# Turning the gated products of the first layer with VectorE and transfers through DRAM, and another order of the first stage's transfers, in a two-layer trunk

## The chip, the cores and the metric

The kernel runs on one core of a Trainium2 chip. The metric is the device time of one execution in microseconds. The engines are named as the profile names them: PE (TensorE, its weight loads apart as PEld), DVE (VectorE), ACT (ScalarE), POOL (GpSimd) and SP (SyncE); the last two only issue transfers here.

## The reference, cut to what matters

One sequence of T = 256 tokens with D = 2048 goes through two layers, all in float32. Layer 0 mixes tokens with an mLSTM, layer 1 with forgetting attention (FoX). Each layer also has a feed-forward part with 5632 hidden columns, and each of the two parts of a layer is preceded by a normalisation that is modulated by numbers worked out from a conditioning vector c:

```python
cs = jax.nn.silu(c)
for layer in range(DEPTH):
    mod = cs @ ada_w[layer] + ada_b[layer]
    sh1, sc1, g1, sh2, sc2, g2 = split(mod, 6)
    h = rms_norm(x, norm_mix_w[layer]) * (1.0 + sc1) + sh1
    y = mlstm_mixer(h) if layer == 0 else fox_mixer(h)
    x = x + g1 * y
    h = rms_norm(x, norm_ffn_w[layer]) * (1.0 + sc2) + sh2
    g, u = jnp.split(h @ w_gate_up[layer], 2, axis=-1)
    x = x + g2 * ((jax.nn.silu(g) * u) @ w_down[layer])
return rms_norm(x, final_norm_w)
```

The change touches two places: how silu(g) * u, which comes out with tokens on the partitions, gets its hidden columns onto the partitions for the product with w_down in layer 0; and the first stage, where mod, h and the first product with the mixer's weights are begun.

## The kernel before, in words

**Matmuls.** Every weight matrix is read once, in tiles of 4 rows of 128 (k) by 512 columns, 1 MB each, by `fetch` (L252) on SP's queue into one of five buffers (`rawp`). To keep float32 accuracy each tile is split, two rows at a time: ACT casts the high part (`hi`, L261), DVE subtracts it from the tile for the low part (`lo`, L262), and PE does three matmuls for each row and each half of the tokens: high activations by high weights (L288), high by low (L289), low by high (L290). Such a split of two rows feeds 12 matmuls; its two results have four buffers each. The activations lie as tiles with the contracted dimension on the partitions, a high part in the first 256 columns and a low one in the next 256.

**Modulation.** The 2 x 6 x 16 rows of `ada_w` come in tiles of 1 MB (L192) on the same queue and into the same five buffers; DVE multiplies each with silu(c) and sums it (L193). In the first stage the tiles for the scale and the shift of layer 0's first norm are taken in the order written there; all later ones are background work (`want`, `bg`), released by a credit that grows at each fetched weight tile by the stage's rate. Gate rows are turned and broadcast over the partitions through DRAM by POOL's queue (`grow`, L402 and L410).

**Steps.** Small work is appended to a list, `steps`, and `tick`, which runs once per fetched weight tile (4 rows of k), takes one step from it. `drain` takes several at once.

**The feed-forward part (`ffn`).** The hidden columns are taken in 11 groups of 512, in two chunks: groups 0 to 5, then the product with their rows of `w_down`, then groups 6 to 10 and the rest of `w_down`. In a group (`swiglu`) the gate column goes through Silu on ACT (L1116), the up column's product is taken by DVE from PSUM (L1119), and then come the steps that turn the 256 x 512 result into four activation tiles, in two halves by `flip(0)` and `flip(1)`: a copy of the high part by ACT (L1147) and a subtraction for the low part by DVE (L1148). How these two see the turned data differs by layer. In layer 0 `turned` does four 128 x 128 transposes on PE into a PSUM bank (L345) in each flip. In layer 1 (`TURN`) six steps stand in place of two: `turn(0)` and `turn(1)`, each a DVE transpose of 32 x 32 squares in place (L1128) with a 256 KB store to DRAM (`aside`) on POOL's queue (L1132); `spread`, four loads from there that set the squares in place (L1136, into `whole`); an empty step; and the two flips, which read SBUF.

In layer 0 the first halves (in k) of 11 columns of the first chunk have been summed before the norm was complete (`nsplit`), so a group there has four ticks; otherwise it has eight. At the end of a chunk `ffn` runs what is left of the steps: all of them in layer 0, all but three in layer 1. The rest goes with the ticks of the product with `w_down`, before whose last fetched tile the list is emptied.

**The first stage.** The first four columns of the mixer's input product (`FIRST`) begin while the modulation is still being worked out. For the first three rows of k the weights and activations are used whole (`full_k`, L785, 16 matmuls for each row), from pairs of rows of 512 KB (`fetch_pair`, L780); the fourth row is split (`split_last`, L797 and L798). `early` is a generator that goes from modulation tile to modulation tile: `upto(k)` runs it until the norm's row k - 1 is written. `norm_full` writes such a row: DVE scales (L737), ACT adds the shift (L741), ACT and DVE split it (`split_act`, L362 and L363).

Of the kernel before, what the change touches and what calls it, by code (L numbers as in the profile page):

```python
# [9 lines left out]
F32 = mybir.dt.float32  # L10
# [3 lines left out]
ALU = mybir.AluOpType  # L14
# [4 lines left out]
T = 256  # L19
# [12 lines left out]
def kernel(  # L32
# [5 lines left out]
    nc = tc.nc  # L38
# [77 lines left out]
    hT = const.tile([P, KT, 2 * T], F32R, name="hT")  # L116
# [72 lines left out]
    def ada_tile(layer, vec, k):  # L189
        j = 16 * vec + k  # L190
        raw = rawp.tile([P, D], F32, tag="raw", name=nm("ada"))
        nc.sync.dma_start(raw, ada_w[layer, j])  # L192
        nc.vector.scalar_tensor_tensor(  # L193
            out=raw, in0=raw, scalar=1.0, in1=cs, op0=ALU.mult, op1=ALU.mult,
            accum_out=acc[layer][:, j : j + 1],
        )
# [164 lines left out]
    def split_act(src, dst):  # L361
        nc.scalar.copy(dst[:, :T], src)  # L362
        nc.vector.tensor_tensor(dst[:, T:], src, dst[:, :T].bitcast(F32), op=ALU.subtract)  # L363
# [366 lines left out]
    FIRST, N2 = CFG["first"], CFG["n2"]  # L730
    full = {}

    def norm_full(k):
        a = mods[0][:, 16 * SC1 + k : 16 * SC1 + k + 1]
        b = mods[0][:, 16 * SH1 + k : 16 * SH1 + k + 1]
        t1 = t256()
        nc.vector.scalar_tensor_tensor(  # L737
            out=t1, in0=xT[k], scalar=a, in1=R, op0=ALU.mult, op1=ALU.mult
        )
        full[k] = f = t256()  # L740
        nc.scalar.activation(f, t1, AF.Identity, bias=b)  # L741
        split_act(f, hT[:, k, :])

    def early():
        for k in range(KT):
            for vec in (SC1, SH1):
                ada_tile(0, vec, k)
                if k == 0 and vec == SC1:
                    row_scale()
                set_mods(0, vec, k, 1)  # L750
                if vec == SC1:
                    yield
            if k < 4:
                norm_full(k)
            else:
                norm_tile(k, 0, SC1, SH1)
            at[0] = k + 1
            yield

    at = [0]  # L760
    gen = early()

    def upto(k):
        while at[0] < k:
            next(gen)
# [12 lines left out]
    def fetch_pair(i, k):  # L778
        raws[i, k // 2] = raw = slot().rearrange("p (k c) -> p k c", c=512)
        nc.sync.dma_start(raw, w[COLS[i] // 512, 0, :, k : k + 2, :])  # L780

    def full_k(k):
        for i in range(FIRST):
            for t in range(2):
                nc.tensor.matmul(  # L785
                    vbanks[i][t], full[k][:, t * P : (t + 1) * P], raws[i, k // 2][:, k % 2, :],
                    start=k == 0, stop=False, skip_group_check=True,
                )

    def split_last(i):  # L790
        if i % 2 == 0:
            fine[i // 2] = [
                splitp.tile([P, 2, 512], F32R, tag=g, name=nm(g)) for g in ("hi", "lo")
            ]
        hi, lo = (h[:, i % 2, :] for h in fine[i // 2])
        src = raws[i, 1][:, 1, :]
        nc.scalar.copy(hi, src)  # L797
        nc.vector.tensor_tensor(lo, src, hi.bitcast(F32), op=ALU.subtract)  # L798
        pairs.append((hi, lo))

    fine, pairs = {}, []
    upto(1)
    for i in range(FIRST):
        fetch_pair(i, 0)
    full_k(0)
    upto(2)
    full_k(1)
    upto(3)
    for i in range(2):
        fetch_pair(i, 2)  # L810
        split_last(i)
    upto(4)
    for i in range(2, FIRST):
        fetch_pair(i, 2)
        split_last(i)
    full_k(2)
    for i in range(FIRST):
        mm_a(vbanks[i], *pairs[i], h_act(3), False, True)
# [248 lines left out]
    begun = project_out(w_out, res, LR[4], 1, 8, norm, gate_up[0], [0, DFF, 512])  # L1067


    TURN = (1,)  # L1070

    def pair(t):
        return t.rearrange("p (t c) -> p t c", t=2)
# [321 lines left out]
```

## Time and profile before

| | |
|---|---|
| median of 3 runs | 2287.39 us (2287.02 to 2288.49) |
| the profiled execution | 2287.58 us |
| its span in the trace | 2285.6 us |
| granted TensorE clock, mean | 0.999 |
| DMA, mean over the span | 278 GB/s, 635.44 MB |
| the first matmuls of L288 | from 44.59 us |
| products (L1119) of layer 0's first chunk | 563.52 to 690.44 us |
| products of layer 0's second chunk | the last transposes after it end at 1044.9 us |

Times in the rows of a view are microseconds from the start of the span. A row of a timeline has the start, the duration, the engine, the line, the operation, the tile written and the tiles read, and how many instructions in a row it stands for; in brackets is the idle time of the engine before it and what ended this. A row of the groups has the busy time, the mean of one in ns, and the idle time before all of them. PE's matmuls overlap, so the duration of one is longer than the step from one to the next.

### The profile page before, as it was taken

The page shows a single profiled execution, that of the slowest core. Times are in us where ns is not written, and L with a number is a line of the kernel's source. Part 1 is how long each engine was busy: PE and PEld are TensorE (multiplying, and loading weights), DVE is VectorE, ACT ScalarE, POOL GpSimd, SP SyncE. Part 2 cuts the span into 40 slices and gives each one's busy share as a digit, 9 for nine tenths or more (in the row PEclk, how much of TensorE's full clock was granted, in tenths as well). Part 3 has the DMA queues.
Part 4 walks back from the last instruction along what each step waited for, and adds up shares of the span by engine and source line. Part 5 has one row for each costly group of instructions (what it writes and reads, how often), then busy time and mean ns, then how long its engine had stood idle before and what let it go on. Part 6 is the DMA issues. An engine that isn't in the chain of part 4 may idle for free.

```text
span 2285.6 us, 26531 instructions
## 1 busy us (share of the span) xinstructions
PE 2259.6 (99%) x10290; PEld 1853.0 (81%) x10290; DVE 1642.5 (72%) x1855; ACT 1133.3 (50%) x1493; POOL 53.8 (2%) x106
## 2 busy tenths in 40 slices
PE   8999999999999999999999999999999999999998
PEld 4877878888888888888888888888888888888886
DVE  7998789878877877865687777777666555555564
ACT  4778564555543344444554544455444443444443
POOL 1000000000000000000000000000010100010000
PEclk9999999999999999999999999999999999999999
DMA  9998989798888889985567878675787665566662
GB/s 386 369 354 332 350 307 355 281 342 336 324 330 332 323 332 342 340 299 185 212 251 277 310 261 293 240 271 195 256 288 254 221 204 189 198 226 217 206 228 104
DMA packets 91809, 635.44 MB, mean 278 GB/s; under 512 B 10962, under 2 KB 11410, under 8 KB 17316
## 3 DMA queue, kind: packets, MB, share of 16 engines
q1 hardware_dynamic: 86400, 617.79, 73.9%
q0 software_dynamic: 5136, 15.83, 2.4%
q8 instruction: 80, 1.31, 0.2%
q14 instruction: 45, 0.37, 0.0%
q10 hardware_dynamic: 148, 0.14, 0.0%
HBM read 625.82 MB, written 7.90 MB: 277 GB/s over the span
## 4 chain that ended last, share of the span: by engine, by line
PE 87%; DVE 6%; DMA 4%; ACT 2%; issue 1%; SPq 0%; POOL 0%; ACTq 0%; DVEq 0%; POOLq 0%
PE mm L290 25%; PE mm L289 25%; PE mm L288 25%; PE mm L271 5%; DMA ada<-in_ada_w_dram 3%; DVE ada L193 3%; PE mm L274 3%; DVE lo L262 2%; ACT hi L261 1%; PE aux L345 1%; PE aux L974 0%; PE aux L483 0%; PE aux L1201 0%; PE mm L554 0%; PE mm L550 0%
## 5 line engine op out<-in xcount | busy, mean ns | idle before, releaser
L262 DVE TENSOR_TENSOR lo<-raw,hi 128x1024 fp32r<-128x1024 f32 x764 | 925.7, 1223 | 488.6 <-ACT hi L261 487.9
L261 ACT CAST hi<-raw 128x1024 fp32r<-128x1024 f32 x764 | 795.6, 1052 | 881.3 <-PE mm L290 780.7
L289 PE MATMUL mm<-lo,hT 128*128 128x512 f32 x1846 | 721.1, 391 | 4.5 <-DVE lo L262 4.5
L288 PE MATMUL mm<-hi,hT 128*128 128x512 f32 x1846 | 720.4, 392 | 1.3 <-ACT hT L362 1.3
L290 PE MATMUL mm<-hi,hT 128*128 128x512 f32 x1846 | 720.8, 390 | 0.0
L193 DVE SCALAR_TENSOR_TENSOR ada<-ada,cs 128x2048 f32<-128x2048 f32 x192 | 438.9, 2286 | 52.4 <-DMA ada<-in_ada_w_dram 52.0
L289 PEld LDWEIGHTS mm<-lo,hT 128*128 128x128 f32 x1846 | 346.9, 188 | 79.1 <-DVE lo L262 8.6
L288 PEld LDWEIGHTS mm<-hi,hT 128*128 128x128 f32 x1846 | 346.6, 188 | 73.5 <-ACT hT L362 2.1
L290 PEld LDWEIGHTS mm<-hi,hT 128*128 128x128 f32 x1846 | 346.7, 188 | 72.7 <-issue 0.5
L288 PE MATMUL mm<-hi,slot 128*128 128x512 f32 x960 | 375.5, 391 | 0.2 <-ACT slot L1007 0.2
L289 PE MATMUL mm<-lo,slot 128*128 128x512 f32 x960 | 374.6, 390 | 0.0
L290 PE MATMUL mm<-hi,slot 128*128 128x512 f32 x960 | 374.6, 391 | 0.0
L290 PEld LDWEIGHTS mm<-hi,slot 128*128 128x128 f32 x960 | 180.3, 188 | 37.8 <-issue 0.7
L288 PEld LDWEIGHTS mm<-hi,slot 128*128 128x128 f32 x960 | 180.3, 188 | 37.7 <-ACT slot L1007 0.8
L289 PEld LDWEIGHTS mm<-lo,slot 128*128 128x128 f32 x960 | 180.4, 188 | 36.9
L271 PE MATMUL mm<-hT,hi 128*128 128x512 f32 x512 | 181.8, 402 | 0.9 <-DVE slot L357 0.9
L274 PE MATMUL mm<-hT,lo 128*128 128x256 f32 x512 | 138.4, 281 | 0.0
L271 PEld LDWEIGHTS mm<-hT,hi 128*128 128x128 f32 x512 | 94.5, 188 | 20.8 <-DVE slot L357 1.3
L274 PEld LDWEIGHTS mm<-hT,lo 128*128 128x128 f32 x512 | 96.8, 189 | 3.1
L829 ACT ACTIVATE slot<-mm 128x512 f32<-128x512 f32 x78 | 45.2, 595 | 39.2 <-PE mm L290 37.4
L1148 DVE TENSOR_TENSOR slot<-slot,slot 128x512 fp32r<-128x512 f32 x22 | 23.8, 1089 | 24.1 <-ACT slot L1147 24.1
L433 ACT ACTIVATE t<-X 128x512 f32<-128x512 f32 x32 | 20.1, 629 | 38.4 <-DVE X L428 38.4
(220 smaller groups left out, 1034.1 us busy)
## 6 DMA issues: line engine op xcount, KB each, us to landing
ada<-in_ada_w_dram SPq DMA_DIRECT2D x192, 1024.0 KB, 6.5
raw<-in_gate_up_dram SPq DMA_DIRECT2D x176, 1024.0 KB, 5.0
raw<-in_down_dram SPq DMA_DIRECT2D x88, 1024.0 KB, 4.8
raw<-in_fox_in_dram SPq DMA_DIRECT2D x48, 1024.0 KB, 4.9
raw<-in_w_in_dram SPq DMA_DIRECT2D x44, 1024.0 KB, 7.4
raw<-in_w_out_dram SPq DMA_DIRECT2D x16, 1024.0 KB, 6.5
raw<-in_fox_out_dram SPq DMA_DIRECT2D x16, 1024.0 KB, 4.9
aside<-slot POOLq DMA_DIRECT2D x22, 256.0 KB, 2.7
```

The costliest lines, as they stand in the source:

```text
L193: nc.vector.scalar_tensor_tensor(out=raw, in0=raw, scalar=1.0, in1=cs, op0=ALU.mult, op1=ALU.mult, accum_out=acc[layer][:, j : j + 1],)
L261: nc.scalar.copy(hi, raw[:, j : j + 2, :])
L262: nc.vector.tensor_tensor(lo, raw[:, j : j + 2, :], hi.bitcast(F32), op=ALU.subtract)
L271: nc.tensor.matmul(ps, hi, rhs, start=first, stop=last, skip_group_check=True)
L274: nc.tensor.matmul(ps[:, T:], lo, rhs[:, :T], start=False, stop=False, skip_group_check=True)
L288: nc.tensor.matmul(ps, a, hi, start=first, stop=False, skip_group_check=True)
L289: nc.tensor.matmul(ps, a, lo, start=False, stop=False, skip_group_check=True)
L290: nc.tensor.matmul(ps, b, hi, start=False, stop=last, skip_group_check=True)
L345: nc.tensor.transpose(ps[:, j * T + t * P : j * T + (t + 1) * P], src[:, t, (2 * i + j) * P : (2 * i + j + 1) * P], ident,)
L433: nc.scalar.activation(t512(), X[:, t, 512 * i : 512 * (i + 1)], AF.Square, accum_out=self.ss[:, t, i : i + 1],)
L829: nc.scalar.activation(SP[i][:, t, :], banks[t], func)
L1148: nc.vector.tensor_tensor(dst[:, :, T:], ps, dst[:, :, :T].bitcast(F32), op=ALU.subtract)
```

## The change

It does two things. First, `TURN` holds both layers: layer 0's gated products are turned by DVE and through DRAM as layer 1's are, with six steps a group in place of two, and three steps are left over at the end of a chunk. Second, the first stage is written in another order. The second and third pairs of modulation tiles are asked for between the first weight pairs rather than behind all four of them, and the next ones between the pairs of the third and fourth row. The low parts of the first rows of the norm are put off (`lows`, `lower`) behind the next modulation tile on DVE, and `split_last` becomes `high_last` and `low_last`. The new file's lines move: what was L1116, L1119, L1128, L1132, L1136, L1147 and L1148 is now L1137, L1140, L1149, L1153, L1157, L1168 and L1169; L780 and L785 are L791 and L796, L797 and L798 are L807 and L811, and the subtraction of `norm_full` is L744 in place of L363.

SP's queue at the start, from the second modulation tile pair's predecessors on (`ada` are modulation tiles, `slot` the weight pairs), before and now:

```order
L780 DMA slot_242<-in_w_in_dram 128x1024
L780 DMA slot_244<-in_w_in_dram 128x1024
L780 DMA slot_246<-in_w_in_dram 128x1024
L780 DMA slot_248<-in_w_in_dram 128x1024
L192 DMA ada_258<-in_ada_w_dram 128x2048
L192 DMA ada_262<-in_ada_w_dram 128x2048
L192 DMA ada_280<-in_ada_w_dram 128x2048
L192 DMA ada_284<-in_ada_w_dram 128x2048
L780 DMA slot_294<-in_w_in_dram 128x1024
L780 DMA slot_300<-in_w_in_dram 128x1024
L192 DMA ada_304<-in_ada_w_dram 128x2048
L192 DMA ada_308<-in_ada_w_dram 128x2048
```

```order
L791 DMA slot_241<-in_w_in_dram 128x1024
L791 DMA slot_243<-in_w_in_dram 128x1024
L192 DMA ada_245<-in_ada_w_dram 128x2048
L791 DMA slot_250<-in_w_in_dram 128x1024
L192 DMA ada_252<-in_ada_w_dram 128x2048
L791 DMA slot_261<-in_w_in_dram 128x1024
L192 DMA ada_279<-in_ada_w_dram 128x2048
L192 DMA ada_284<-in_ada_w_dram 128x2048
L791 DMA slot_293<-in_w_in_dram 128x1024
L192 DMA ada_295<-in_ada_w_dram 128x2048
L791 DMA slot_300<-in_w_in_dram 128x1024
L192 DMA ada_308<-in_ada_w_dram 128x2048
```

The third and fourth modulation tile stood behind four weight pairs and now behind two and three; the fifth and sixth keep their place, and the seventh stands ahead of the second pair of the third row.

DVE at the same place, around the third row of the norm (L737), before and now:

```order
L193 SCALAR_TENSOR_TENSOR ada_284,acc_124<-ada_284,cs 128x2048
L187 TENSOR_TENSOR mods_122<-acc_124,prm 128x1
L737 SCALAR_TENSOR_TENSOR t_47_288<-slot_130,mods_122,R 128x256
L363 TENSOR_TENSOR hT<-t_48_290,hT 128x256
L798 TENSOR_TENSOR lo_297<-slot_294,hi_296 128x512
L798 TENSOR_TENSOR lo_297<-slot_300,hi_296 128x512
L193 SCALAR_TENSOR_TENSOR ada_304,acc_124<-ada_304,cs 128x2048
```

```order
L193 SCALAR_TENSOR_TENSOR ada_284,acc_124<-ada_284,cs 128x2048
L187 TENSOR_TENSOR mods_122<-acc_124,prm 128x1
L737 SCALAR_TENSOR_TENSOR t_47_288<-slot_130,mods_122,R 128x256
L193 SCALAR_TENSOR_TENSOR ada_295,acc_124<-ada_295,cs 128x2048
L744 TENSOR_TENSOR hT<-t_48_290,hT 128x256
L181 SCALAR_TENSOR_TENSOR mods_122<-acc_124,prm 128x1
L811 TENSOR_TENSOR lo_303<-slot_293,hi_302 128x512
```

The next modulation tile (L193) comes ahead of the row's low part, and ahead of the low parts of the first two weight rows (L798, now L811).

DVE at the end of layer 0's first chunk: the products of group 5 (L1119, now L1140) and the flips around them (L1148, now L1169). `lo` are weights' low parts; in the second piece `slot_4982` and `slot_5152` are the turned data of groups 3 and 4, `slot_4984` and `slot_5154` the products of groups 4 and 5:

```order
L262 TENSOR_TENSOR lo_5443<-raw_5440,hi_5442 128x1024
L262 TENSOR_TENSOR lo_5447<-raw_5440,hi_5446 128x1024
L193 SCALAR_TENSOR_TENSOR ada_5545,acc_125<-ada_5545,cs 128x2048
L1119 TENSOR_TENSOR slot_5167<-mm_5271,slot_5167 128x512
L1119 TENSOR_TENSOR slot_5167<-mm_5272,slot_5167 128x512
L262 TENSOR_TENSOR lo_5480<-raw_5477,hi_5479 128x1024
L262 TENSOR_TENSOR lo_5484<-raw_5477,hi_5483 128x1024
L1148 TENSOR_TENSOR slot_5422<-aux_5423,slot_5422 128x2x256
L1148 TENSOR_TENSOR slot_5430<-aux_5431,slot_5430 128x2x256
```

```order
L262 TENSOR_TENSOR lo_5443<-raw_5440,hi_5442 128x1024
L193 SCALAR_TENSOR_TENSOR ada_5474,acc_125<-ada_5474,cs 128x2048
L1169 TENSOR_TENSOR slot_5410<-slot_4982,slot_5410 128x2x256
L1169 TENSOR_TENSOR slot_5413<-slot_4982,slot_5413 128x2x256
L1149 STREAM_TRANSPOSE slot_5151<-slot_4984 128x4x4x32 x2
L262 TENSOR_TENSOR lo_5447<-raw_5440,hi_5446 128x1024
L1140 TENSOR_TENSOR slot_5154<-mm_5248,slot_5154 128x512
L1140 TENSOR_TENSOR slot_5154<-mm_5249,slot_5154 128x512
L262 TENSOR_TENSOR lo_5480<-raw_5477,hi_5479 128x1024
L262 TENSOR_TENSOR lo_5484<-raw_5477,hi_5483 128x1024
L193 SCALAR_TENSOR_TENSOR ada_5551,acc_125<-ada_5551,cs 128x2048
L262 TENSOR_TENSOR lo_5517<-raw_5514,hi_5516 128x1024
```

Before, no squares stand there and a flip reads PSUM (`aux`). Now the flips of group 3 and the squares of group 4 (L1149) stand ahead of the second split of the first tile of `w_down` (`lo_5447`), and group 4's flips come six rows after that tile's last, behind the products of group 5.

The diff:

```diff
--- before.py
+++ after.py
@@ -739,12 +739,23 @@
         )
         full[k] = f = t256()
         nc.scalar.activation(f, t1, AF.Identity, bias=b)
-        split_act(f, hT[:, k, :])
+        dst = hT[:, k, :]
+        nc.scalar.copy(dst[:, :T], f)
+        lows.append(lambda: nc.vector.tensor_tensor(
+            dst[:, T:], f, dst[:, :T].bitcast(F32), op=ALU.subtract
+        ))
+
+    lows = []
+
+    def lower():
+        while lows:
+            lows.pop(0)()
 
     def early():
         for k in range(KT):
             for vec in (SC1, SH1):
                 ada_tile(0, vec, k)
+                lower()
                 if k == 0 and vec == SC1:
                     row_scale()
                 set_mods(0, vec, k, 1)
@@ -787,32 +798,42 @@
                     start=k == 0, stop=False, skip_group_check=True,
                 )
 
-    def split_last(i):
+    def high_last(i):
         if i % 2 == 0:
-            fine[i // 2] = [
+            fine.append([
                 splitp.tile([P, 2, 512], F32R, tag=g, name=nm(g)) for g in ("hi", "lo")
-            ]
-        hi, lo = (h[:, i % 2, :] for h in fine[i // 2])
-        src = raws[i, 1][:, 1, :]
-        nc.scalar.copy(hi, src)
-        nc.vector.tensor_tensor(lo, src, hi.bitcast(F32), op=ALU.subtract)
-        pairs.append((hi, lo))
-
-    fine, pairs = {}, []
+            ])
+        pairs.append([h[:, i % 2, :] for h in fine[-1]])
+        nc.scalar.copy(pairs[i][0], raws[i, 1][:, 1, :])
+
+    def low_last(i):
+        hi, lo = pairs[i]
+        nc.vector.tensor_tensor(lo, raws[i, 1][:, 1, :], hi.bitcast(F32), op=ALU.subtract)
+
+    fine, pairs = [], []
     upto(1)
-    for i in range(FIRST):
+    for i in (0, 1):
         fetch_pair(i, 0)
+    next(gen)
+    fetch_pair(2, 0)
+    next(gen)
+    fetch_pair(3, 0)
     full_k(0)
-    upto(2)
     full_k(1)
     upto(3)
-    for i in range(2):
+    fetch_pair(0, 2)
+    next(gen)
+    fetch_pair(1, 2)
+    for i in (0, 1):
+        high_last(i)
+        low_last(i)
+    next(gen)
+    assert at[0] == 4
+    lower()
+    for i in (2, 3):
         fetch_pair(i, 2)
-        split_last(i)
-    upto(4)
-    for i in range(2, FIRST):
-        fetch_pair(i, 2)
-        split_last(i)
+        high_last(i)
+        low_last(i)
     full_k(2)
     for i in range(FIRST):
         mm_a(vbanks[i], *pairs[i], h_act(3), False, True)
@@ -1067,7 +1088,7 @@
     begun = project_out(w_out, res, LR[4], 1, 8, norm, gate_up[0], [0, DFF, 512])
 
 
-    TURN = (1,)
+    TURN = (0,1)
 
     def pair(t):
         return t.rearrange("p (t c) -> p t c", t=2)
```

## The prediction

> **What bounds the kernel now.** I read the busy times of the whole execution first, then a table of four stretches.
>
> ```profile
> PE 2259.6 (99%) x10290; PEld 1853.0 (81%) x10290; DVE 1642.5 (72%) x1855; ACT 1133.3 (50%) x1493; POOL 53.8 (2%) x106
> 563.50:690.40 126.90, 126.22 (x577) 104.16 (x575) 101.11 (x102) 64.11 (x80) 1.58 (x3) 1.00 0.89 332
> 875.00:1045.00 170.00, 170.00 (x770) 140.58 (x768) 123.03 (x118) 72.23 (x78) 1.57 (x3) 1.00 0.85 311
> 1640.00:1675.00 35.00, 34.19 (x149) 27.52 (x147) 24.49 (x24) 17.98 (x19) 3.47 (x6) 1.00 0.74 241
> 18.00:45.00 27.00, 21.58 (x50) 9.18 (x50) 18.68 (x27) 4.94 (x12) 0.00 (x0) 1.00 1.02 418
> ```
>
> The columns of the four lower lines are the stretch and its length, then PE, its weight loads, DVE, ACT and POOL busy, the granted clock, the DMA share and GB/s. TensorE works 99% of the span, so time is saved by taking work from PE or by filling its few gaps, and lost by making PE wait. The first stretch is layer 0's first chunk of gated products (6 groups), the second part of its second chunk (5 groups), the third a piece of layer 1's first chunk, which already uses the turning by DVE, and the fourth the start. DVE is free for 25.8 us of the first stretch (126.90 − 101.11) and 47 of the second. At the start the DMA engines are full, and PE is not.
>
> **The part by part account: what PE loses.** Next the groups of instructions (busy us, mean ns of one, idle before), then PE's timeline around one batch of transposes, and two subtractions on DVE in a stretch where only PE's pace releases them.
>
> ```profile
> L262 DVE TENSOR_TENSOR lo<-raw,hi 128x1024 fp32r<-128x1024 f32 x764 | 925.7, 1223 | 488.6 <-ACT hi L261 487.9
> L193 DVE SCALAR_TENSOR_TENSOR ada<-ada,cs 128x2048 f32<-128x2048 f32 x192 | 438.9, 2286 | 52.4 <-DMA ada<-in_ada_w_dram 52.0
> L1147 ACT CAST slot<-slot 128x512 fp32r<-128x512 f32 x22 | 24.1, 1108 | 16.3 <-DMA slot<-aside 16.3
> L1148 DVE TENSOR_TENSOR slot<-slot,slot 128x512 fp32r<-128x512 f32 x22 | 23.8, 1089 | 24.1 <-ACT slot L1147 24.1
> L1128 DVE STREAM_TRANSPOSE slot<-slot 128x512 f32<-128x512 f32 x22 | 23.5, 1080 | 0.0
> L345 PE MATMUL aux<-ident,slot 128*128 128x128 f32 x120 | 17.6, 273 | 1.5 <-DVE slot L1119 1.5
> L1148 DVE TENSOR_TENSOR slot<-aux,slot 128x512 fp32r<-128x512 f32 x22 | 14.9, 684 | 0.0
> ```
>
> ```profile
> 569.26 0.60 PE L345 MATMUL aux<-ident,slot 128*128 128x128 f32 x4
> 569.62 0.47 PE L288 MATMUL mm<-hi,hT 128*128 128x512 f32 x1
> 569.93 0.39 PE L289 MATMUL mm<-lo,hT 128*128 128x512 f32 x1
> ```
>
> ```profile
> 1662.40 1.23 DVE L262 TENSOR_TENSOR lo<-raw,hi 128x1024 fp32r<-128x1024 f32 x1 [1.50 <-ACT hi L261]
> 1665.12 1.23 DVE L262 TENSOR_TENSOR lo<-raw,hi 128x1024 fp32r<-128x1024 f32 x1 [1.49 <-ACT hi L261]
> ```
>
> The change takes 88 of the 120 transposes of L345 away: 11 groups, two flips each, four to a flip. Their 273 ns overlap, so I price a batch by when the next work starts: 569.26 to 569.62 is 0.36 us, and the matmul after it follows 0.31 us later where 0.23 is the usual step (a split of the weights, 12 matmuls, takes PE 2.72 us, the distance of the two subtractions), so 0.08 more. That makes 0.44 us, 22 batches, **9.7 us**. The one PE wait of the L345 row, 1.5 us for the product of L1119, goes too: **−11.2 us** in all. The second chunk's share, ten batches or 4.4 us, is nearly sure, as PE is busy 170.00 of 170.00 there and DVE has the room.
>
> **The start.** Views: PE's and DVE's timelines.
>
> ```profile
> 18.34 5.42 PE L785 MATMUL mm<-slot,t 128*128 128x512 f32 x12 [1.08 <-ACT t L741]
> 28.22 0.48 DVE L737 SCALAR_TENSOR_TENSOR t<-slot,mods,R 128x256 f32<-128x256 f32 x1
> 29.29 5.42 PE L785 MATMUL mm<-slot,t 128*128 128x512 f32 x12 [3.82 <-ACT t L741]
> 36.26 5.34 PE L785 MATMUL mm<-slot,t 128*128 128x512 f32 x12
> 39.62 0.30 PEld L785 LDWEIGHTS mm<-slot,t 128*128 128x128 f32 x2 [0.59 <-DMA slot<-in_w_in_dram]
> 44.59 0.51 PE L288 MATMUL mm<-hi,hT 128*128 128x512 f32 x1 [1.26 <-ACT hT L362]
> ```
>
> From 18.34 to 44.59 PE spends 26.25 us, with idle of 3.82 and 1.26. The 3.82 ends with the second row of the norm (DVE's L737 at 28.22), whose two modulation tiles stand behind all four first weight pairs on SP. Now one comes ahead of two of these pairs and one ahead of the last: with 0.5 to 1 MB less in front at 418 GB/s (1.2 to 2.4 us) I put L737 1.2 us earlier, at 27.0, and PE's block at 28.0 instead of 29.29. The block of the third row then follows at 35.0. But the pairs of the third row have the same bytes ahead of them as before, and the DMA share is 1.02, so the third one still lands at about 39.6, where PE waits for it now (0.59). Eight of that block's 16 matmuls then remain, 3.5 us: it ends near 43.1, where 44.59 stood: 1.5 earlier. The subtraction deferred behind a modulation tile is 0.1 to 0.5 us of work that no longer delays that tile; it must be there by the first L288. I take **−1.4 us**, between 0 and 2.5 (nothing, or the 1.26 before the first L288 too, less what ACT's casts need).
>
> **What DVE, ACT and POOL get.** A group now costs DVE two squares of 1.080 us, and its two subtractions read SBUF where they read PSUM: 1.089 against 0.684. That is 2.16 + 0.81 = 2.97 us a group, 17.8 for the first chunk's six, against 25.8 free, of which the shorter stretch (six groups' transposes, 5.3, and the 1.5 wait) takes 6.8 away. So DVE has 1 us left in 120 there: all waits for DMA have to fit into work of others. ACT's cast costs 1.108, and ACT is half idle, but it waits in its queue for the transfer, and behind it stand the casts of the weights (L261). DVE's subtraction of the flip stands behind the cast, and behind that the low halves of the weights (L262), for which PE waits. POOL's queue gets five waiting issues a group, beside the row broadcasts.
>
> The transfers' way, from the end of the second square to ACT's cast, is priced by layer 1:
>
> ```profile
> 1640.88 4.62 DVE L262 TENSOR_TENSOR lo<-raw,hi 128x1024 fp32r<-128x1024 f32 x4
> 1645.40 1.29 DVE L1119 TENSOR_TENSOR slot<-mm,slot 128x512 f32<-128x512 f32 x2
> ...
> 1648.65 1.07 DVE L1128 STREAM_TRANSPOSE slot<-slot 128x512 f32<-128x512 f32 x1
> ```
>
> ```profile
> 1658.29 2.34 POOL L1136 DMA_DIRECT2D slot<-aside  x4 [7.71 <-DMA aside<-slot]
> 1669.67 1.10 ACT L1147 CAST slot<-slot 128x512 fp32r<-128x512 f32 x1 [3.00 <-DMA slot<-aside]
> 1694.81 1.08 DVE L1128 STREAM_TRANSPOSE slot<-slot 128x512 f32<-128x512 f32 x1
> 1712.10 1.10 ACT L1147 CAST slot<-slot 128x512 fp32r<-128x512 f32 x1 [1.17 <-DMA slot<-aside]
> 1820.68 1.99 DVE L1128 STREAM_TRANSPOSE slot<-slot 128x512 f32<-128x512 f32 x2
> 1833.78 2.11 ACT L1147 CAST slot<-slot 128x512 fp32r<-128x512 f32 x2 [1.87 <-DMA slot<-aside]
> 2168.83 2.00 DVE L1128 STREAM_TRANSPOSE slot<-slot 128x512 f32<-128x512 f32 x2
> 2183.68 2.12 ACT L1147 CAST slot<-slot 128x512 fp32r<-128x512 f32 x2 [3.62 <-DMA slot<-aside]
> ```
>
> In these four ACT waited for the transfer, so they show its full length, call it L: 1649.72 to 1669.67 is 19.9, then 16.2, 11.1 (1822.67 to 1833.78) and 12.9.
>
> **Where that wait reaches PE.** In the first chunk a group's six steps meet four ticks, so they pile up, and DVE's order at the chunk's end has the flips of groups 3, 4 and 5 with only a few subtractions between a group's squares and its flips. I walk it from P, the product of group 4, which PE leaves with 13 splits (35.4 us) to go until the second split of the down-projection.
>
> Instructions in a row overlap a little: a subtraction is 1.15 us (4.62 for four), a product 0.6 (1.29 for two), a modulation tile 2.2 by the same overlap, a square or a flip 1.0. From P on DVE does 2 products, 6 subtractions, 2 tiles, a flip and 2 squares: 1.2 + 6.9 + 4.4 + 1.0 + 1.9 = 15.4, with 1.1 for a wait for weights 16.6. Then come the transfer of group 3, ACT's cast 1.1, two flips 2.0, group 4's squares 1.9, and the subtraction PE needs 1.1: it is ready at P + 22.7 + L and needed at P + 35.4. **First wait: L − 12.7.** Likewise for group 4: its squares end 1.1 before that point, the same cast, flips, squares and subtraction follow, and PE needs them five splits (13.6) later: **second wait: L − 8.6**, never below 1.6, as DVE's other work between (products, four subtractions, two tiles: 10.2) must be done too. For group 5, with four splits (10.9) and one flip: **third wait: L − 9.9**, never below 0.4.
>
> For group 3, in a stretch with a 0.89 DMA share, its squares apart as in the two longer rows and row broadcasts ahead of it on POOL, I take L = 16.2; for the other two, whose squares run together as in the two shorter rows, 12.0, between these rows. That gives 3.5 + 3.4 + 2.1 = **9.0 us**, with ends of 3.9 (12.9, 11.1, 11.1) and 21.1 (19.9, 16.2, 16.2). The piece of layer 1 with L = 19.9 lost only 0.81 of PE (35.00 − 34.19), as its flips lie further behind.
> The other groups of the first chunk and the second chunk have 13 to 19 us of DVE work between square and flip: **+1.0**, between 0 and 2.
>
> **The sum.** The profiled execution took 2287.58 us, its span 2285.6, the median of the runs 2287.39, which is 0.19 less. 2287.58 − 11.2 − 1.4 + 9.0 + 1.0 = 2285.0; less 0.19 it is **2284.8**. The likeliest case's own range is 2281 to 2289.
>
> **The rivals.**
> *The transfers are hidden.* If L is 7 to 11 for all three, the waits fall to their floors or to 3.9, and the other groups to 0: 2276.8 to 2278.7. For it: the mean times from issue to landing,
>
> ```profile
> aside<-slot POOLq DMA_DIRECT2D x22, 256.0 KB, 2.7
> slot<-aside POOLq DMA_DIRECT2D x44, 128.0 KB, 5.5
> ```
>
> 2.7 + 5.5 and the issues (2.34 for four, after the store) make 10.5. Against it: the four lengths above, all longer. The Trainium skill ("DMA: Bandwidth & Descriptors", section "Anatomy of one DMA — SWDGE (gpsimd) path") has a transfer from this queue cost about 2.0 us and its bytes over 436 GB/s: by it, as an estimate, the store takes 2.6 and a spread 2.3, L is about 7, and only floors remain; the 2.7 of the store agrees, the 5.5 of the spread doesn't. Chance 0.31.
> *The waits are long: slower.* With the queues full, every L is 17, between the two longer rows: 4.3 + 8.4 + 7.1 = 19.8, and 2295.6; at 19.9 each 28.5, and 2304.3. It decides against the change (over 2292.0) when the three lengths add up to 47.4, 15.8 each. For it: the chunk's DMA share of 0.89 against 0.74 where layer 1 saw 19.9. Against it: the shorter two of four rows. Chance 0.18.
> *DVE itself becomes the bound.* If its gaps in the first chunk can't be used (they end when a tile lands or a weight buffer frees), all 17.8 us show: 2287.58 − 12.6 + 17.8 − 0.19 = 2292.6. Against it: 488.6 us of DVE's idle time stand before L262, waiting for ACT's cast, and work before it would slide into them. The Trainium skill ("VectorE: DVE Perf Modes", section "Rules for kernel authors") gives a 128×128 transpose to TensorE if its result may lie in PSUM, the reverse of this change; the trace has four at 0.44 us on PE and 2.97 us of DVE for eight, so the rule holds where PE isn't the bound. Chance 0.04.
> *The start gains nothing*, as the transfers there are bound by their bytes: 2286.2. Chance 0.05.
> That the transposes aren't taken away is excluded: PE's order has no L345 of layer 0's gated products left.
>
> **How the numbers follow.** The forecast has 0.42, of which 0.05 lies below 2282.8. About 0.2%, 4.6 us, is what a measurement can tell from no change, so "same" is 2282.8 to 2292.0. Faster: 0.31 + 0.05 = 0.36; same: 0.37 + 0.05 = 0.42; slower: 0.18 + 0.04 = 0.22. The range, 2277 to 2295, leaves out half of the slow case (0.09) and a little of the hidden one.
>
> **What would show it.** Between 640 and 700 us PE should have three waits for L262's subtractions or ACT's flips, 2 to 4 us each, and ACT waits for "aside" before its casts (L1168 now); PE busy without gaps in layer 0's second chunk, 4 us shorter; the first L288 near 43.1. It is wrong if ACT never waits there (the hidden case), if one wait is over 6 us (the long one), or if DVE is busy without PE's waits lying behind flips (DVE's bound).

## The result, and the profile after

The changed kernel takes 2309.83 us (median of 4 runs, 2308.61 to 2314.83) against 2287.69 us of the kernel before on the same chip (4 runs): the ratio is 1.0104, with a 95% interval of 1.0088 to 1.0120. The profiled execution took 2310.0 us, 22.4 more than that of before. The forecast was 2284.8 us, between 2277 and 2295: it was wrong, and the slower case, to which 0.22 was given, is what happened, harder than it was priced.

The busy times of the page of the changed kernel, and two stretches and three single slices of it (length, then PE, its weight loads, DVE, ACT and POOL busy, the granted clock, the DMA share, GB/s):

```profile
PE 2259.1 (98%) x10202; PEld 1847.8 (80%) x10202; DVE 1668.0 (72%) x1877; ACT 1144.2 (50%) x1493; POOL 92.3 (4%) x172
560.00:745.00 185.00, 164.04 (x700) 132.75 (x699) 144.88 (x145) 84.83 (x96) 22.46 (x39) 0.96 0.90 324
690.00:700.00 10.00, 0.80 (x1) 0.29 (x1) 4.47 (x5) 5.59 (x6) 0.69 (x2) 0.69 0.18 44
700.00:710.00 10.00, 9.30 (x34) 7.59 (x35) 10.00 (x10) 2.41 (x3) 2.79 (x5) 0.79 0.94 300
720.00:730.00 10.00, 9.44 (x34) 7.63 (x35) 8.59 (x10) 2.11 (x2) 2.66 (x5) 0.83 0.87 284
875.00:1060.00 185.00, 177.49 (x764) 145.30 (x763) 141.89 (x138) 79.09 (x81) 15.57 (x27) 0.97 0.93 335
```

The same two stretches in the kernel before:

```profile
560.00:745.00 185.00, 183.54 (x834) 151.76 (x833) 148.48 (x152) 86.26 (x102) 1.58 (x3) 1.00 0.88 329
875.00:1060.00 185.00, 185.00 (x835) 152.98 (x834) 130.77 (x125) 78.44 (x84) 1.57 (x3) 1.00 0.82 299
```

PE has 88 instructions fewer, and yet it stands for 20.96 us in the 185 around layer 0's first chunk, where it stood for 1.46 before, and for 7.51 in the 185 of the second, which had no gap before. DVE has about as much room as before in the first, and 11 us less in the second (141.89 busy in place of 130.77). New is the clock column: it falls to 0.79 and 0.83 in slices in which PE works. PE's timeline has the largest stops:

```profile
697.51 0.80 PE L288 MATMUL mm<-hi,slot 128*128 128x512 f32 x1 [8.38 <-ACT hi L261]
700.70 0.80 PE L289 MATMUL mm<-lo,slot 128*128 128x512 f32 x1 [2.39 <-DVE lo L262]
...
720.56 0.50 PE L289 MATMUL mm<-lo,slot 128*128 128x512 f32 x1 [4.39 <-DVE lo L262]
...
735.70 0.50 PE L288 MATMUL mm<-hi,slot 128*128 128x512 f32 x1 [2.58 <-ACT slot L1168]
...
1006.41 0.79 PE L288 MATMUL mm<-hi,hT 128*128 128x512 f32 x1 [4.49 <-ACT hi L261]
```

The first four are the three waits that the prediction placed at the end of the first chunk, in their order. The last is one that it did not have. What PE waits for are the weights' casts and subtractions, and what these wait for is seen in the order of the first stop: DVE's second square of group 3, POOL's store, POOL's loads, ACT's cast and DVE's flip, from the timelines of these engines:

```profile
670.77 1.07 DVE L1149 STREAM_TRANSPOSE slot<-slot 128x512 f32<-128x512 f32 x1
672.13 0.55 POOL L1153 DMA_DIRECT2D aside<-slot  x1 [1.50 <-DVE slot L1149]
683.83 2.35 POOL L1157 DMA_DIRECT2D slot<-aside  x4 [11.15 <-PE mm L290]
694.41 2.10 ACT L1168 CAST slot<-slot 128x512 fp32r<-128x512 f32 x2 [15.06 <-DMA slot<-aside]
695.53 2.10 DVE L1169 TENSOR_TENSOR slot<-slot,slot 128x512 fp32r<-128x512 f32 x2 [12.72 <-ACT slot L1168]
```

From 671.84 to 694.41 are 22.6 us: 11.7 from the store's issue to that of the loads, 10.6 for these. The row of the loads names PE, but the second store takes 11.0 us from issue to landing (672.13 to 683.17), so it is the store that they wait for. ACT's 15.06 and DVE's 12.72 are idle time in which the next weights could have been split, but their instructions stand behind the flip. By 694 the DMA engines are almost idle too (0.18): SP issues no load between 682.84 and 700.67, which fits buffers full of weights that nobody splits. The squares and casts of groups 4, 5 and, at the chunk's beginning, 0:

```profile
697.56 2.04 DVE L1149 STREAM_TRANSPOSE slot<-slot 128x512 f32<-128x512 f32 x2
714.28 2.11 ACT L1168 CAST slot<-slot 128x512 fp32r<-128x512 f32 x2 [5.40 <-DMA slot<-aside]
717.43 2.03 DVE L1149 STREAM_TRANSPOSE slot<-slot 128x512 f32<-128x512 f32 x2
734.56 2.12 ACT L1168 CAST slot<-slot 128x512 fp32r<-128x512 f32 x2 [3.05 <-DMA slot<-aside]
...
565.18 1.06 DVE L1149 STREAM_TRANSPOSE slot<-slot 128x512 f32<-128x512 f32 x1
588.00 2.11 ACT L1168 CAST slot<-slot 128x512 fp32r<-128x512 f32 x2 [8.24 <-DMA slot<-aside]
```

The transfers took 14.7, 15.1 and 21.8 us. At the start the first split matmul comes earlier, and the third row's weights land when they did:

```profile
39.48 1.98 PE L796 MATMUL mm<-slot,t 128*128 128x512 f32 x4 [1.22 <-DMA slot<-in_w_in_dram]
...
42.62 0.79 PE L288 MATMUL mm<-hi,hT 128*128 128x512 f32 x1
```

42.62 against 44.59 is a gain of 2.0 us, of which 1.6 are left ahead of layer 0's gated products (a subtraction of L262 there begins at 555.32 in place of 556.95).

### The profile page after: what moved, and what is told of

Same layout as the page of the kernel before. It is cut to its first block, busy times and chain, and to the rows that moved or that the text cites. A ratio compares the mean times of both kernels' runs of the same rounds, so it can differ in the third digit from the quotient of the medians.

```text
span 2308.2 us, 26463 instructions
## 1 busy us (share of the span) xinstructions
PE 2259.1 (98%) x10202; PEld 1847.8 (80%) x10202; DVE 1668.0 (72%) x1877; ACT 1144.2 (50%) x1493; POOL 92.3 (4%) x172
## 4 chain that ended last, share of the span: by engine, by line
PE 83%; DVE 6%; DMA 6%; ACT 2%; issue 2%; POOL 0%; SPq 0%; ACTq 0%; DVEq 0%; POOLq 0%
PE mm L289 23%; PE mm L290 23%; PE mm L288 23%; PE mm L271 5%; DVE lo L262 3%; PE mm L274 3%; DVE ada L193 2%; DMA slot<-aside 2%; DMA raw<-in_gate_up_dram 1%; DMA ada<-in_ada_w_dram 1%; DMA aside<-slot 1%; ACT hi L261 1%; DMA slot<-in_w_in_dram 1%; PE aux L483 1%; PE aux L995 0%
## 5 line engine op out<-in xcount | busy, mean ns | idle before, releaser
L262 DVE TENSOR_TENSOR lo<-raw,hi 128x1024 fp32r<-128x1024 f32 x764 | 921.7, 1221 | 435.0 <-ACT hi L261 434.4
L288 PE MATMUL mm<-hi,hT 128*128 128x512 f32 x1846 | 719.2, 392 | 7.7 <-ACT hi L261 7.7
L193 DVE SCALAR_TENSOR_TENSOR ada<-ada,cs 128x2048 f32<-128x2048 f32 x192 | 438.7, 2285 | 52.7 <-DMA ada<-in_ada_w_dram 52.6
L288 PEld LDWEIGHTS mm<-hi,hT 128*128 128x128 f32 x1846 | 347.3, 188 | 81.6 <-ACT hi L261 9.0
L288 PE MATMUL mm<-hi,slot 128*128 128x512 f32 x960 | 376.7, 392 | 11.1 <-ACT hi L261 8.4
L288 PEld LDWEIGHTS mm<-hi,slot 128*128 128x128 f32 x960 | 181.1, 189 | 49.9 <-ACT hi L261 8.8
L1169 DVE TENSOR_TENSOR slot<-slot,slot 128x512 fp32r<-128x512 f32 x44 | 47.6, 1090 | 74.4 <-ACT slot L1168 74.4
L1153 POOL DMA_DIRECT2D aside<-slot x44 | 24.8, 564 | 1508.1 <-DVE slot L1149 1054.1
L1168 ACT CAST slot<-slot 128x512 fp32r<-128x512 f32 x44 | 48.0, 1108 | 66.1 <-DMA slot<-aside 66.1
```

The lines of the kernel that those rows point to most:

```text
L193: nc.vector.scalar_tensor_tensor(out=raw, in0=raw, scalar=1.0, in1=cs, op0=ALU.mult, op1=ALU.mult, accum_out=acc[layer][:, j : j + 1],)
L262: nc.vector.tensor_tensor(lo, raw[:, j : j + 2, :], hi.bitcast(F32), op=ALU.subtract)
L288: nc.tensor.matmul(ps, a, hi, start=first, stop=False, skip_group_check=True)
L1153: nc.gpsimd.dma_start(aside[t], squares[:, t, :])
L1168: nc.scalar.copy(dst[:, :, :T], ps)
L1169: nc.vector.tensor_tensor(dst[:, :, T:], ps, dst[:, :, :T].bitcast(F32), op=ALU.subtract)
```

## The experiments

The theory formed from this trace (W): the transfers through DRAM take 15 to 23 us in layer 0, ACT's and DVE's queues stand behind them, PE runs out of split weights, and its clock falls after the longer stops. The rivals: DVE's added work is what costs (D), the transfers' traffic itself delays the weights (T), the new order of the start costs time further on (S).

**The two parts apart.** One kernel is the kernel before with the turning alone, the other the changed kernel with the turning taken back:

```diff
-    TURN = (1,)
+    TURN = (0,1)
```

> The kernel before with only the first layer's turning changed, the first stage as it was. Theory W (ACT and DVE stand in their queues behind the transfers through DRAM, PE runs out of split weights, and its clock falls after the longer stops): the whole loss comes from the turning, and the first stage gave 2.0 us (first split matmuls at 42.6 in place of 44.6), so about 2312 us, 2.0 above the changed kernel. Rival S (the other order of the first stage costs time further on): below 2309 us.

> The changed kernel with the turning taken back, so only the first stage's order is new. Theory W: 2.0 us below the kernel before, about 2285.7. Rival S: not below it.

Measured: 2311.9 us for the turning alone, where the kernel before took 2287.77 (1.0109, 1.0082 to 1.0137), and 2286.31 for the start alone (0.9994, 0.9985 to 1.0003). All the loss is the turning's; the start's 2.0 us are in the trace, and its time agrees without proving them. S falls.

**Without the wait.** Layer 0's flips read the squares, and the second kernel also sends the loads to a DRAM buffer in place of a slot:

```diff
-                squares = pair(slot())
-                whole = slot().rearrange("p (t m) -> p t m", m=4)
+                flat = slot()
+                squares = pair(flat)
+                whole = (slot() if layer else dram.tile([P, 1024], ...)).rearrange(...)
...
-                    ps = whole[:, :, 2 * i : 2 * i + 2].rearrange("p t m -> p m t")
+                    src = flat.rearrange("p (t m) -> p t m", m=4) if layer == 0 else whole
+                    ps = src[:, :, 2 * i : 2 * i + 2].rearrange("p t m -> p m t")
```

> The changed kernel, but in layer 0 the flips read the squares as DVE left them and not what the transfers bring back, so the data that goes on is in the wrong places; all squares, stores and loads are still made, and nothing waits for the loads. Theory W: the waits go and the clock stays up, so the gains are left alone: 2287.7 - 11.2 - 2.0 and 1 to 3 for DVE's added work, about 2276. Theory D (DVE's added work is what costs): still above 2300. If the mere traffic of the transfers delays the weights: in between, 2285 to 2300.

> As the run without the wait (flips read the squares, data in the wrong places), but layer 0's loads go to another DRAM buffer in place of an SBUF slot: the same traffic, no wait for it, and no slot that is held until a load has landed. In the earlier run one slot was still waited for: ACT stood 11.9 us before a flip until a load into the slot's old tile had landed, and PE 5.2. Theory W: with that gone too only the gains and DVE's added work are left, 2274 to 2280. Rival T (the transfers' traffic itself delays the weights): about 2287 again. Theory D (DVE's added work): the same or above.

The first took 2287.17 us, between W and D, and its ACT shows why (a cast that reads only squares, yet waits for a load):

```profile
704.27 1.09 ACT L1170 CAST slot<-slot 128x512 fp32r<-128x512 f32 x1 [11.94 <-DMA slot<-aside]
```

Its flip writes a slot that an earlier group's load had not yet left: the run had taken one wait away and kept another. With the loads sent elsewhere it is 2274.72 us against 2286.53 (0.9956, 0.9941 to 0.9971), as W had it, with the same bytes. PE's stretch of the first chunk in that kernel:

```profile
560.00:745.00 185.00, 184.68 (x814) 152.17 (x813) 166.48 (x165) 94.87 (x105) 22.04 (x39) 1.00 0.97 371
```

DVE works 166 of the 185 us here and the DMA share is 0.97, more than in the changed kernel, and PE stands for only 0.32 us: neither D nor T holds.

**DVE's work alone.** Layer 0 turned by PE, and DVE does two squares for each of its groups into a slot that nobody reads:

```diff
...
+            def both(i):
+                if layer == 0:
+                    idle_turn(i)
+                flip(i)
...
-            steps.extend([lambda: flip(0), lambda: flip(1)])
+            steps.extend([lambda: both(0), lambda: both(1)])
```

> The first stage in its new order, layer 0 turned by PE as before, and beside it DVE does the two squares of each layer 0 group into a spare slot that nobody reads (22 squares, 23.8 us of DVE work added; no store, no load, no wait). Theory W: DVE has room for it, 2286 to 2290. Theory D: 12 us or more above the run with the new first stage alone, so 2298 or more.

2284.61 us against 2286.53 (0.9992, 0.9982 to 1.0001): 23.8 us of added work cost nothing that can be measured. D is refuted a second time, here for the squares alone; the slower subtractions of the flips are in the kernel with the loads sent elsewhere.

**What makes the transfers long.** During the first chunk the modulation tiles bring a quarter of their bytes:

```diff
-        nc.sync.dma_start(raw, ada_w[layer, j])
+        n = 512 if light else D
+        nc.sync.dma_start(raw[:, :n], ada_w[layer, j, :, :n])
...
-            out=raw, in0=raw, scalar=1.0, in1=cs, op0=ALU.mult, op1=ALU.mult,
+            out=raw, in0=cs if light else raw, scalar=1.0, in1=cs, op0=ALU.mult, op1=ALU.mult,
```

> The changed kernel, but the modulation tiles that are fetched during layer 0's first chunk bring a quarter of their bytes (DVE multiplies as many numbers as before, of other data). Theory W, with the length of a transfer set by the loads that SP has in flight: the transfers of the first chunk take 8 to 12 us in place of 15 to 23, its PE waits (about 21 us and 5 of lowered clock) go nearly all, the second chunk keeps its own (7.5 and some 3): about 2288. If the transfer's length is its own and not the traffic's: above 2303. Theory D: above 2303 too, with PE waiting behind DVE at work.

2299.91 us (1.0047, 1.0030 to 1.0063), between the two. Its five executions lie far apart (2292.18 to 2303.62), and the trace is of the shortest. The stretch of the first chunk, and group 3's second square and cast:

```profile
560.00:745.00 185.00, 174.58 (x740) 141.40 (x739) 153.20 (x155) 89.48 (x99) 22.47 (x39) 0.97 0.75 248
...
672.17 1.07 DVE L1151 STREAM_TRANSPOSE slot<-slot 128x512 f32<-128x512 f32 x1
685.73 2.16 ACT L1170 CAST slot<-slot 128x512 fp32r<-128x512 f32 x2 [5.16 <-DMA slot<-aside]
```

Group 3's transfer takes 12.5 us in place of 22.6 (groups 4 and 5: 13.3 and 11.6), and PE's gaps there fall from 20.96 to 10.42. So SP's loads set most of the length for group 3; but at a DMA share of 0.75 a remainder of 12 us is left, and it stops PE as well. W's number for this run, that nearly all waits would go, was wrong. One more thing lies beside group 3's stores in the changed kernel: two 512 KB broadcasts of gate rows, issued on the same queue at 666.23, whose median to landing is 9.9 us. Group 0, which has none near it, took 21.8 us all the same; no run takes the broadcasts away, so their share in the 22.6 stays open.

**The second chunk alone.** Groups 6 to 10 through DRAM, 0 to 5 through PE:

```diff
-            if layer in TURN:
+            turning = layer == 1 or gr >= 6
+            if turning:
...
```

> The changed kernel with the turning in layer 0 for groups 6 to 10 alone; groups 0 to 5 go through PE as before. Theory W: the three flips at the first chunk's end and the two in its beginning are gone, so the 21 us of PE stops and 5 us of lowered clock there too; the second chunk gains 4.4 on PE and loses what its own stops cost, 7.5 and some 3 of clock as in the changed kernel's profile, or little as in the run with light tiles: 2282 to 2293. If the loss doesn't depend on the place: half of it remains, about 2297.

2283.31 us (0.9983, 0.9974 to 0.9992), at the lower end, and slightly faster than the kernel before. The transfers of groups 6 to 8 take 20 to 21 us here as well, and ACT waits up to 4.15 us for them, but PE stands for only 1.19 us in the stretch from 875 to 1060, where it stood for 7.51 in the changed kernel. So the second chunk's loss isn't set by the transfers' length alone; why the same code lost more behind a disturbed first chunk is not shown.

**The flips later.** Squares and stores in one step, flips a group later, the loads into the slot of the product; the second kernel does so for the second chunk alone:

```diff
+            if layer == 0:
+                steps.extend([lambda: (turn(0), turn(1)), spread] + held)
+                held[:] = [lambda: flip(0), lambda: flip(1)]
+                return
...
```

> The changed kernel with other places for the flips in layer 0: a group's two squares and stores go in one step, its loads in the next, and its flips come behind the next group's loads, some 6 ticks (33 us) after its squares; the last group's flips come at the fourth and fifth tick of the product with w_down. The loads land in the slot of the product, so no slot more is held. Same work, same traffic, same DVE. Theory W: the transfers of 15 to 23 us lie wholly beside other work, but for the last group of a chunk (0 to 3 us each): 2275 to 2282. Theories D and T: above 2295.

> The first chunk of layer 0 through PE as before, the second chunk (groups 6 to 10) through DRAM with late flips, the first stage in its new order. Theory W: the run with the turning in the second chunk alone lost 1.2 us of PE to one flip there; with late flips none, so the kernel before less 2.0 less 4.4: 2279 to 2281, about 2 below that run.

The first took 2285.37 us (0.9995, 0.9985 to 1.0004), some 24 less than the changed kernel with the same work, but not 2275 to 2282. PE has no stop left in the second chunk but two of 0.3 and 0.5; in the first, group 5 is late:

```profile
687.01 1.99 DVE L1150 STREAM_TRANSPOSE slot<-slot 128x512 f32<-128x512 f32 x2
709.38 1.09 ACT L1169 CAST slot<-slot 128x512 fp32r<-128x512 f32 x1 [11.32 <-DMA slot<-aside]
```

20.4 us after its squares ACT gets its data, and PE stands for 4.5 us. Another stop there, 2.2 us near 655, lies behind no flip: DVE waited 2.66 us for a modulation tile, and this tile, a product and two squares stood ahead of the subtraction that PE needed. The kernel with late flips in the second chunk alone took 2282.85 us (0.9982, 0.9972 to 0.9991). Its profile has PE busy for 185.00 of 185 us there, as expected, but its time is not measurably below that of the run without the late flips (2283.31), where 2 us were expected; so small a difference lies within the intervals of both.

**The last groups through PE.** The late flips with group 5 through PE (`gr != 5`), and then with groups 4 and 5:

```diff
+            turning = layer == 1 or gr not in (4, 5)
+            if turning:
...
```

> The run with the late flips, and the last group of layer 0's first chunk (group 5) turned by PE as before; in the run before this one it was that group alone whose transfer (20.4 us from its squares to ACT's cast) stopped PE for 4.5 us and lowered its clock. Everything else of that run stands, the second chunk with all five groups through DRAM. Theory W: the kernel before, less 2.0 at the start, less 10.3 (20 of 22 batches of transposes and the wait for the product), plus 1 to 4 for DVE's stricter order in the first chunk: 2275 to 2280. If another transfer takes that group's place as the late one: 2283 or more.

> The run with the late flips, with groups 4 and 5 of layer 0's first chunk turned by PE as before, and groups 0 to 3 and 6 to 10 through DRAM with late flips; the last flips that wait for a transfer (group 3's) stand about 23 DVE instructions behind their squares, and none falls into the time in which POOL's queue also has the gate rows' store and broadcast. Theory W: the kernel before, less 2.0 at the start, less 9.4 (18 of 22 batches of transposes, 7.9, and the wait for the product), plus 0 to 3 for DVE's stricter order: 2275 to 2279. If the transfers' length grows with any distance that is left to them: 2283 or more.

The first is a miss: 2290.91 us against 2286.21 (1.0021, 1.0009 to 1.0033). The other case named above came true: another transfer had become the late one, that of group 4. POOL's queue, and ACT's cast:

```profile
661.96 0.61 POOL L1159 DMA_DIRECT2D slot<-aside  x1 [7.34 <-ACT hi L261]
662.57 0.50 POOL L402 DMA_DIRECT2D row<-t  x1
663.06 1.18 POOL L1159 DMA_DIRECT2D slot<-aside  x2
669.46 1.13 POOL L410 DMA_DIRECT2D slot<-row  x2 [5.22 <-DMA row<-t]
670.58 0.62 POOL L1159 DMA_DIRECT2D slot<-aside  x1
...
682.40 2.10 ACT L1170 CAST slot<-slot 128x512 fp32r<-128x512 f32 x2 [15.48 <-DMA slot<-aside]
```

Three of its loads are out by 664.2; the fourth waits until 670.58 behind the gate rows' broadcast, which itself waits for its store. ACT gets the data at 682.40, and PE stands for 11.5 us. With that group through PE too the time is 2276.77 us against 2287.02 (0.9953, 0.9938 to 0.9968): less than both kernels, and as expected. The stretch of the first chunk, group 3's squares and first cast, and the transfers (count, KB each, median us from issue to landing) in that kernel:

```profile
560.00:745.00 185.00, 185.00 (x825) 153.04 (x824) 159.84 (x160) 93.64 (x105) 15.53 (x27) 1.00 0.97 359
...
630.59 2.03 DVE L1151 STREAM_TRANSPOSE slot<-slot 128x512 f32<-128x512 f32 x2
660.82 1.12 ACT L1170 CAST slot<-slot 128x512 fp32r<-128x512 f32 x1
...
aside<-slot POOLq DMA_DIRECT2D x8, 256.0 KB, 6.3
slot<-aside POOLq DMA_DIRECT2D x16, 128.0 KB, 8.7
```

The transfers are no shorter than in the changed kernel (there 4.9 and 8.0 in the same stretch). They lie beside 28.2 us of other work, so no cast waits, and PE has no gap. A small part of the gain isn't the late flips': in this kernel the steps left at the first chunk's end go with the ticks of the product with `w_down` and not all at once. The kernel with late flips in the second chunk alone does so too, and its first chunk, all through PE, is 0.8 to 1.6 us shorter for it (262.2 us from the 169th to the 263rd subtraction of L262, the first ahead of its products and the second behind its last flips, against 263.8 in the kernel before and 263.0 with the start alone).

## Why the prediction was wrong, point by point

**The transposes, −11.2: right.** From the 169th to the 361st subtraction of L262, which is from ahead of layer 0's gated products to behind their last flips, the kernel before takes 534.7 us and the kernel with the loads sent elsewhere 523.4, so 11.3 less with all of DVE's added work in it.

**The start, −1.4: right,** 2.0 at the first L288 and 1.6 further on; the norm's second row was scaled at 26.62, where 27.0 was forecast, and the third row's weights landed at 39.48, where 39.6 was forecast.

**The waits at the first chunk's end, +9.0: the mechanism right, the size wrong.** This is the first term that failed. The walk gave L − 12.7, L − 8.6 and L − 9.9; with the lengths that were measured, 22.6, 14.7 and 15.1, these give 9.9 + 6.1 + 5.2 = 21.2, and the stops were 10.8, 4.4 and 2.6, together 17.7. What was wrong are the three L, taken as 16.2, 12.0 and 12.0 from layer 1. The prediction compared the DMA share of long stretches (0.89 and 0.74), and these don't sort the rows: the 12.9 lies in a stretch of 0.74 too (2165 to 2190 us). Over the transfers' own time the share is 0.97, 0.93, 0.91 and 0.85 for the lengths 19.9, 16.2, 11.1 and 12.9, and in the changed kernel 0.98 to 1.01 for the seven of 18 to 22 us and 0.94 and 0.88 for the two behind the long stop, 14.7 and 15.1; only group 3, with the broadcasts beside its stores and 22.6 at 0.90, stands out. In the kernel before it is 0.95 from 660 to 690 us, so the rows to take for group 3 were 16.2 to 19.9, and none of them reaches 22.6.

**The other groups, +1.0: wrong, 10.7.** The reason given was that 13 to 19 us of DVE work lie between square and flip. But the same transfers take 18 to 22 us there as well (21.8 for group 0), so most of these flips stopped ACT (8.24 us for group 0, 3.00 for group 1, none for group 2, 1.25 to 6.39 for groups 6 to 9), and PE stood for 3.2 us in the first chunk (20.96 − 17.74) and 7.5 in the second, the longest of 4.49. The bound, 0 to 2, has no row beside it; by the prediction's own 16.2 and 19.9 a distance of 13 to 19 us was not safe.

**The clock, absent from the sum: 7.6, as an estimate.** Before and behind PE's return to its pace, after the stop at 700.70:

```profile
703.00 0.63 PE L288 MATMUL mm<-hi,slot 128*128 128x512 f32 x1
703.43 0.63 PE L289 MATMUL mm<-lo,slot 128*128 128x512 f32 x1
...
704.90 0.39 PE L288 MATMUL mm<-hi,slot 128*128 128x512 f32 x1
705.12 0.40 PE L289 MATMUL mm<-lo,slot 128*128 128x512 f32 x1
```

The steps are 0.43 us and then 0.22. Eight or nine matmuls run so after each of the four stops near 700, 720, 957 and 1007. The granted clock is 0.50 from 693.87 to 704.11, 721.17 to 724.58, 956.69 to 960.10 and 1004.48 to 1011.31; PE works 4.21, 3.41, 3.27 and 4.38 us in these, 15.3 in all, and at half the pace half of that is lost. No stop of the kernel before had shown it: the prediction's widest one, 3.82 us at the start, was followed by matmuls at their usual duration.

**The account.** The stops are 20.96 + 7.51 = 28.5 us; with 7.6 for the clock and 11.3 gained, layer 0's gated products and what follows them should be 24.8 us longer. From the 169th to the 361st subtraction of L262 they are 26.8 longer (561.5 against 534.7), so 2.0 us have no place in this account. The start's 1.6 go off, and behind the 361st subtraction 2.5 more: there the code is the same in both, and in the other runs that part is from 1.3 us shorter to 3.9 longer than in the kernel before. What is left is 22.7, and the two profiled executions differ by 22.4.

**The rivals.** The long waits were the right rival, and its point of decision held: the three lengths add up to 52.4, over 47.4, and one wait, 10.8, was over 6 us. But it had neither the other groups nor the clock, so its own 2295.6 to 2304.3 was too low as well. The transfers are not hidden: the 2.7 and 5.5 us, which are medians over the whole kernel and not means, don't hold beside layer 0's loads. The Trainium skill's sum of a fixed 2.0 us and the bytes over 436 GB/s ("DMA: Bandwidth & Descriptors", section "Anatomy of one DMA — SWDGE (gpsimd) path") gave, as the prediction's estimate, a length of about 7, and none that ACT waited for in any trace here is below 10.1. DVE as the bound is refuted by the kernel with the loads sent elsewhere, which has all of DVE's added work and no loss. The rule that the prediction cites, a transpose to PE where the result may lie in PSUM, is not borne out as a rule of time either: with the flips late enough, 18 of the 22 batches are cheaper through DVE and DRAM.

## What to carry to other kernels

A transfer's length is to be read where the same loads are in flight over the transfer's own time, not as a median or beside the average of a long stretch; then the distance between the work that starts it and the in-order instruction that waits for it must exceed that length, not the usual one. A wait on an engine's queue holds up the work behind it that another engine needs, however idle the engine looks. Where the last piece of a stage has no such distance, leave it on the old path: here nine groups of eleven through DRAM made the kernel 10 us faster, the start's 2 among them, and all eleven, with their flips close behind, 22 slower.

## What the runs showed of the hardware

PE ran at about half its pace for 3 to 4 us after stops of 8.4 + 2.4, 4.4 and 4.5 us, not after one of 2.6; but also after 1.7 and 0.8 us with one matmul between. The Trainium skill ("TensorE: Matmul & The Clock Gate", section "Part 1: The HAM clock gate (the "warmup" mystery)") has the clock halved after an idle window of about 3.4 us that runs freely, and full again after a busy one: the durations agree, but the window needn't be wholly idle. The windows ahead of and in the low clock near 957, and around the stop of 2.6 us:

```profile
953.28:956.69 3.41, 1.04 (x4) 0.30 (x2) 3.00 (x3) 3.41 (x5) 0.00 (x0) 1.00 1.01 420
956.69:960.10 3.41, 3.27 (x8) 2.59 (x9) 3.41 (x4) 1.63 (x2) 0.00 (x0) 0.50 0.64 216
731.41:734.83 3.42, 1.72 (x8) 1.10 (x6) 0.84 (x2) 0.37 (x2) 0.00 (x0) 1.00 0.97 329
734.83:738.24 3.41, 2.54 (x10) 1.88 (x11) 2.56 (x3) 2.81 (x3) 0.00 (x0) 1.00 1.02 423
```

The four low pieces of the changed kernel last 3.41 us or two or three times that. In the 3.41 us ahead of each PE worked for 0.00, 0.61, 1.04 and 0.86 us; with 1.72 around the stop of 2.6 the clock stayed up. So the stops of 1.7 and 0.8 us counted together, as they fell into one window. The limit isn't sharp in these records: in the kernel with the turning alone a window with 1.80 us of work (952.80 to 956.21) was followed by a low one. Stores of 256 KB took 2.7 us in the median of the kernel before; in layer 0's first chunk of the changed kernel stores and loads of this kind took up to 11.0, beside loads of SP's queue that are not related to them. On POOL's queue, in the kernel with group 5 alone through PE, a load waited 6 us behind a broadcast that had nothing to do with it. Not settled is what the remaining 12 us of a transfer consist of when the loads are light.
